# Which expert tiles have their activations worked out ahead: six whole groups, or the first eight tiles and then every third

## The chip, the cores and the metric

The kernel runs on one core of a Trainium2 chip. The metric is the device time of one execution in microseconds (us), lower is better. TensorE (PE) multiplies matrices, VectorE (DVE), ScalarE (ACT) and GpSimd (POOL) work element by element, SyncE (SP) issues most transfers. Each engine takes its own instructions strictly in order and waits on semaphores.

## The reference

Two transformer blocks over 512 tokens of 1024 numbers. The change lies in the expert layer (PEER) of the first block, of which this is the core:

```python
def chunk(xc):                               # 128 tokens at a time
    ...
    idx = jnp.take_along_axis(cidx, fi, axis=-1)     # 8 heads x 16 experts of 16384
    g = jax.nn.softmax(fv, axis=-1)
    u = u_tab[idx]
    a = jax.nn.gelu(jnp.einsum('chkd,cd->chk', u, xc).astype(jnp.float32), approximate=False)
    vv = v_tab[idx]
    return jnp.einsum('chk,chkd->cd', (g * a).astype(vv.dtype), vv)
```

## The kernel before

**Two ways for the experts.** The first 128 tokens are done literally: for each of 128 (head, choice) pairs a row of 1024 numbers per token is gathered from the u table and one from the v table. That makes 256 gathers of 128 rows (512 KB each), issued from POOL (L694) and used on DVE: a u gather by `jk` (L707, a dot product, followed by a short instruction that reads the accumulator), a v gather by `yg` (L709, L711). The other 384 tokens go densely: the 16384 experts are 128 tiles of 128, and for every tile n
- `u_tile(n)` loads 512 KB of the u table, splits it into a high and a low part (`whi` on ACT, L84; `wlo` on DVE, L85), does 24 matmuls (L111) and a Gelu on ACT into a tile `ga` (128 x 384, 192 KB);
- `gated(n)` multiplies `ga` by the gates of its tile on DVE (L755) and splits the product into `wh` (ACT) and `wl` (DVE, L85 too);
- the v part loads 512 KB of the v table, splits it like u, and does 18 matmuls (L782) into six accumulators that stay open over all 128 tiles.

One load and split of 512 KB is called a unit: tile n has a u unit and a v unit. The raw buffers (`wraw`) are a ring of 4 units, `whi` and `wlo` rings of 3.

**Ahead of the loop.** While DVE builds the gate table, PE has room: `ahead(n)` does the u unit of 48 tiles (those of the first six groups of eight). Eight results stay in SBUF (`kept`, tiles 0 to 7), 40 are written to DRAM (`gad`) and read back in the loop by L747, called a reload here. The tiles `ga` are a ring of 8, and a reload into a buffer needs that its last reader is done.

**The loop over n.** Its program order is: v unit of n; u unit or reload of n+2; gates of n+1; v matmuls of n. A scheduler turns that order into a fixed list for each engine at build time, so that instructions of neighbouring tiles interleave. SP's list holds all loads and reloads of the loop: a load that waits for a buffer holds up those behind it. The gates of eight tiles (1536 KB) come by one transfer `gt` from the table `Gd` (L734).

**Pacing the gathers.** After each of the two DVE steps of `gated`, `pace(w, ins)` advances a count by w and lets as many gathers (and, with more than three held, uses) follow `ins` as the count is due:

```python
steps = 8 * VW * GA + 16 * (16 - GA) - 12
...
while done < total * step / steps and gq:
    if len(held) > 3:
        use(ins)
    gather(ins)
    done += 1
```

A tile worked out ahead advances the count by VW = 0.6 in all (two calls of VW/2), any other by 2. `total` is 256.

Of the kernel before, what the change touches and what calls it, by code (L numbers as in the profile page):

```python
# [8 lines left out]
F32 = mybir.dt.float32  # L9
# [11 lines left out]
P = 128  # L21
# [2 lines left out]
KD = D // P  # L24
NTMP = 5
WG = (4, 4, 5)
GAHEAD = 6
KO = (4, 5, 6, 7, 0, 1, 2, 3)
NR = 1
GS = (2, 2, 1, 1)  # L30
# [3 lines left out]
EB, QB, KB, ST = 2, 2, 2, 42  # L34
FA, GA1 = 1.0, 3
SCB = 3
GAB, VW, HB = 8, 0.6, 6
G = 128


# [4 lines left out]
def drain(g):  # L45
    for _ in g:
        pass


class Kern:  # L50
# [383 lines left out]
    def peer(self, h, xg, ss):  # L434

        nc, tc = self.nc, self.tc
        A = self.A
        NB = 3
        ND, T0 = NB * P, P
        TG, NT = 16, NB * P // 16  # L440
        GA = GAHEAD
        st = ExitStack()
        px = st.enter_context(tc.tile_pool(name="px", bufs=1))
        dr = st.enter_context(tc.tile_pool(name="dr", bufs=1, space=DRAM))
        Gd = dr.tile([16, P, NT, 8, TG], F32, name="Gd")
        gad = [dr.tile([P, 8, ND], F32, name=f"gad{n}") for n in range(GA - 1)]
        xtd = px.tile([P, KD, P], F32, name="xtd")
        gid = px.tile([P, P], I32, name="gid")
        gat = px.tile([P, P], F32, name="gat")
# [3 lines left out]
        def ga_tile():  # L453
            return pga.tile([P, ND], F32, name="ga", tag="ga", bufs=GAB)
# [30 lines left out]
        for c in range(2):  # L485
            ps = self.aux().rearrange("p (k d) -> p k d", k=4)
            for k in range(4 * c, 4 * c + 4):
                f = self.t()
# [37 lines left out]
        def route(b):  # L526
# [44 lines left out]
            return terms, g  # L571

        def table(b, terms, g, between):

            rt = rt1
# [42 lines left out]
        def u_tile(n, out):  # L618
            ps = self.mm()[:, :ND]
            self.mm3(ps, self.unit(A["uT"][n], KD), X)  # L620
            nc.scalar.activation(out, ps, AF.Gelu)

        def ahead(n):

            ga, n = ga_tile(), (n + 8) % (GA * 8)
            u_tile(n, ga)
            if n < 8:
                kept.append(ga)
            else:
                nc.sync.dma_start(gad[n // 8 - 1][:, n % 8], ga)  # L630

        kept = []

# [14 lines left out]
        steps, units = 0, 0  # L648
# [3 lines left out]
        def between():  # L652
            nonlocal steps, units
            steps += 1
            if steps in (8, 24):
                routed[steps // 16 + 2] = route(steps // 16 + 2)
            if steps > 32 and steps % 2:
                next(rest, None)
            while units < steps * (GA * 8 - HB) / 48:
                ahead(units)  # L660
                units += 1

        for b in (1, 2, 3):
            table(b, *routed.pop(b), between)
        drain(rest)
        while units < GA * 8:
            ahead(units)
            units += 1
        g_st.close()
# [21 lines left out]
        def gather(after):  # L691
            z, n = gq.pop(0)
            r = pg.tile([P, D], F32, name="gr", tag="gr", bufs=6)
            dep(nc.gpsimd.indirect_dma_start(out=r, out_offset=None, in_=(A["u"], A["v"])[z],  # L694
                                             in_offset=bass.IndirectOffsetOnAxis(ap=gid[:, n:n + 1], axis=0)), after)
            held.append((z, n, r))

        def use(after):
            z, n, r = held.pop(0)
            c = n // 16  # L700
            s16 = slice(16 * c, 16 * c + 16)
            if z == 1 and n % 16 == 0:
                nc.scalar.activation(ag[:, s16], ag[:, s16], AF.Gelu)
                nc.vector.tensor_tensor(ag[:, s16], ag[:, s16], gat[:, s16], op=OP.mult)
            if z == 0:
                jk = pg.tile([P, D], BF, name="jk", tag="jk", bufs=1)
                i = nc.vector.scalar_tensor_tensor(jk, r, 1.0, xf, op0=OP.mult, op1=OP.mult, accum_out=ag[:, n:n + 1])  # L707
            elif n == 0:
                i = nc.vector.tensor_scalar(yg, r, ag[:, n:n + 1], None, op0=OP.mult)  # L709
            else:  # L710
                i = nc.vector.scalar_tensor_tensor(yg, r, ag[:, n:n + 1], yg, op0=OP.mult, op1=OP.add)  # L711
            if after is not None:
                dep(i, after)

        total = len(gq)
        steps = 8 * VW * GA + 16 * (16 - GA) - 12
        done, step = 0, 0.0

        def pace(w, ins):
            nonlocal done, step  # L720
            step += w
# [5 lines that stand above are left out]
# [3 lines left out]
        gts, gas, ws = {}, {}, {}  # L730

        def gates_of(gi):
            gts[gi] = pl.tile([P, NT, 8, TG], F32, name="gt", tag="gt", bufs=2)
            nc.sync.dma_start(gts[gi], Gd[gi])  # L734

        def gelu_u(n):
            gi, i = divmod(n, 8)
            if i == 2 and gi < 15:
                gates_of(gi + 1)
            if n < 8:  # L740
                gas[n] = kept[i]
                return
            ga = gas[n] = ga_tile()
            if gi >= GA:
                u_tile(n, ga)
            else:
                nc.sync.dma_start(ga, gad[gi - 1][:, i])  # L747

        def gated(n):
            gi, i = divmod(n, 8)  # L750
            ga = gas.pop(n)
            wh = pw.tile([P, ND], F32R, name="wh", tag="wh", bufs=3)
            wl = pw.tile([P, ND], F32R, name="wl", tag="wl", bufs=3)
            g3 = ga.rearrange("p (n t) -> p n t", t=TG)
            last = nc.vector.tensor_tensor(g3, g3, gts[gi][:, :, i], op=OP.mult)  # L755
            pace(VW / 2 if gi < GA else 1.0, last)
            last = self.split(ga, wh, wl)
            pace(VW / 2 if gi < GA else 1.0, last)
            ws[n] = wh, wl

        gates_of(0)
        gelu_u(0)
        gelu_u(1)
        gated(0)
        for n in range(P):
            vh, vl = self.unit(A["v"][n * P:n * P + P].rearrange("p (k g) -> p k g", g=G), 8)
            if n + 2 < P:
                gelu_u(n + 2)
            if n + 1 < P:
                gated(n + 1)  # L770
            else:
                assert not gq
                while held:
                    use(None)
                take = self.start2()
            wh, wl = ws.pop(n)
            for f in range(2):
                fs = slice(4 * f, 4 * f + 4)
                for t in range(NB):
                    tk = slice(t * P, t * P + P)  # L780
                    for j, (a, b) in enumerate(((wh, vh), (wh, vl), (wl, vh))):
                        nc.tensor.matmul(acc[f][t], a[:, tk], b[:, fs].rearrange("p k g -> p (k g)"),  # L782
                                         start=n == 0 and j == 0, stop=n == P - 1 and j == 2)
# [917 lines left out]
```

## Time and profile before

| | |
|---|---|
| three timed runs | 2801.33 us median (2794.91 to 2803.78) |
| profiled execution | 2801.58 us, span from first to last instruction 2799.8 us |
| PE busy | 2661.8 us, 95% of the span |
| DVE busy | 1929.1 us, 69% |
| ACT, POOL busy | 1222.7 us, 746.6 us |
| granted TensorE clock, mean | 0.979 of full speed |
| HBM | 158 GB/s over the span |

All times below count from the first instruction of the profiled execution. The expert loop runs from about 770 us to 1679 us. A busy time is that of an engine's instructions; matmuls are pipelined, so the time of a piece of PE work is best read from the start of one piece to the start of the next. "idle before <- X" names what ended an engine's wait.

### The profile page before, as it was taken

The page shows a single profiled execution, that of the slowest core. Times are in us where ns is not written, and L with a number is a line of the kernel's source. Part 1 is how long each engine was busy: PE and PEld are TensorE (multiplying, and loading weights), DVE is VectorE, ACT ScalarE, POOL GpSimd, SP SyncE. Part 2 cuts the span into 40 slices and gives each one's busy share as a digit, 9 for nine tenths or more (in the row PEclk, how much of TensorE's full clock was granted, in tenths as well). Part 3 has the DMA queues.
Part 4 walks back from the last instruction along what each step waited for, and adds up shares of the span by engine and source line. Part 5 has one row for each costly group of instructions (what it writes and reads, how often), then busy time and mean ns, then how long its engine had stood idle before and what let it go on. Part 6 is the DMA issues. An engine that isn't in the chain of part 4 may idle for free.

```text
span 2799.8 us, 38104 instructions
## 1 busy us (share of the span) xinstructions
PE 2661.8 (95%) x13941; PEld 2202.5 (79%) x13941; DVE 1929.1 (69%) x3742; ACT 1222.7 (44%) x2124; POOL 746.6 (27%) x807
## 2 busy tenths in 40 slices
PE   8999999799999999999999998898899989999997
PEld 6777888789987788888888886676667778888886
DVE  4664579997666778887778858877687765545336
ACT  4664354566532333333333336445555545222234
POOL 0100110000022345454545511443544513111002
PEclk9999999899999999999999998999899999999999
DMA  3112322467798878898899952121000013222332
GB/s 122 61 42 76 118 101 84 141 200 241 245 346 288 300 267 324 327 330 314 321 331 332 323 176 91 61 61 46 1 1 1 1 46 107 91 98 91 98 98 76
DMA packets 173356, 446.15 MB, mean 159 GB/s; under 512 B 14192, under 2 KB 76784, under 8 KB 170992
## 3 DMA queue, kind: packets, MB, share of 16 engines
q1 hardware_dynamic: 136304, 309.47, 32.8%
q0 software_dynamic: 36864, 134.23, 13.3%
q8 instruction: 110, 1.80, 0.3%
q14 instruction: 78, 0.64, 0.1%
HBM read 404.33 MB, written 37.22 MB: 158 GB/s over the span
## 4 chain that ended last, share of the span: by engine, by line
PE 69%; DVE 14%; DMA 5%; POOL 4%; issue 4%; ACT 4%; SPq 0%; DVEq 0%; POOLq 0%; ACTq 0%
PE mm L111 46%; PE aux L782 10%; DMA ga<-gad 3%; PE mm L782 2%; DVE wlo L85 2%; PE aux L607 1%; PE mm L1285 1%; PE aux L367 1%; PE aux L325 1%; POOL gl_E L1379 1%; POOL gr L694 1%; PE aux L1212 1%; DVE gl_K L1388 1%; POOL t L915 1%; DMA wraw<-in_v_dram 1%
## 5 line engine op out<-in xcount | busy, mean ns | idle before, releaser
L84 ACT CAST whi<-wraw 128x1024 fp32r<-128x1024 f32 (+2 forms) x439 | 454.1, 1035 | 920.4 <-PE mm L111 764.2
L85 DVE TENSOR_TENSOR wlo<-wraw,whi 128x1024 fp32r<-128x1024 f32 (+2 forms) x439 | 569.1, 1297 | 319.6 <-ACT whi L84 295.9
L111 PE MATMUL mm<-xb,whi 128*128 128x384 f32 (+1 forms) x2656 | 732.8, 356 | 13.9 <-ACT whi L84 13.3
L111 PEld LDWEIGHTS mm<-xb,whi 128*128 128x128 f32 x2656 | 483.6, 190 | 59.2 <-ACT whi L84 28.5
L111 PE MATMUL mm<-xb,wlo 128*128 128x384 f32 (+1 forms) x1328 | 472.8, 356 | 11.7 <-DVE wlo L85 11.7
L694 POOL DMA_INDIRECT gr<-in_u_dram,gid x128 | 192.2, 1501 | 605.3 <-DVE ga L755 495.3
L111 PEld LDWEIGHTS mm<-xb,wlo 128*128 128x128 f32 x1328 | 252.2, 190 | 40.7 <-DVE wlo L85 21.8
L782 PE MATMUL aux<-wlo,wh 128*128 128x512 f32 x640 | 255.4, 399 | 12.3 <-DVE wlo L85 12.2
L694 POOL DMA_INDIRECT gr<-in_v_dram,gid x128 | 194.2, 1517 | 235.3 <-DVE ga L755 106.3
L782 PE MATMUL aux<-whi,wl 128*128 128x512 f32 x640 | 253.4, 396 | 0.0
L782 PE MATMUL aux<-whi,wh 128*128 128x512 f32 x640 | 253.2, 396 | 0.0
L111 PE MATMUL mm<-fx,whi 128*128 128x512 f32 (+1 forms) x736 | 223.2, 386 | 0.0
L111 PE MATMUL mm<-fp,whi 128*128 128x512 f32 (+1 forms) x732 | 200.6, 360 | 1.1 <-ACT fp L84 0.5
L711 DVE SCALAR_TENSOR_TENSOR yg<-gr,ag,yg 128x1024 f32<-128x1024 f32 x127 | 163.1, 1285 | 4.3 <-DMA gr<-in_v_dram,gid 1.8
L707 DVE SCALAR_TENSOR_TENSOR jk<-gr,xtd 128x1024 bf16<-128x1024 f32 x128 | 156.4, 1222 | 9.5 <-DMA gr<-in_u_dram,gid 7.1
L111 PEld LDWEIGHTS mm<-fx,whi 128*128 128x128 f32 x736 | 135.7, 188 | 30.8
L111 PE MATMUL mm<-x,whi 128*128 128x512 f32 x432 | 148.0, 424 | 8.4 <-DVE h L792 7.5
L782 PEld LDWEIGHTS aux<-wlo,wh 128*128 128x128 f32 x640 | 120.5, 188 | 43.1 <-DVE wlo L85 20.0
L111 PEld LDWEIGHTS mm<-fp,whi 128*128 128x128 f32 x732 | 129.6, 189 | 26.3 <-DVE fp L85 1.7
L111 PE MATMUL mm<-fx,wlo 128*128 128x512 f32 (+1 forms) x368 | 141.8, 385 | 0.0
L782 PEld LDWEIGHTS aux<-whi,wl 128*128 128x128 f32 x640 | 120.6, 188 | 24.6
L782 PEld LDWEIGHTS aux<-whi,wh 128*128 128x128 f32 x640 | 120.7, 189 | 24.4
(491 smaller groups left out, 4703.4 us busy)
## 6 DMA issues: line engine op xcount, KB each, us to landing
wraw<-in_uT_dram SPq DMA_DIRECT2D x128, 512.0 KB
wraw<-in_v_dram SPq DMA_DIRECT2D x128, 512.0 KB
wraw<-in_w_in_dram SPq DMA_DIRECT2D x57, 512.0 KB
Gd<-stg SPq DMA_DIRECT2D x24, 1024.0 KB
gt<-Gd SPq DMA_DIRECT2D x16, 1536.0 KB
wraw<-in_ffn_gate_dram SPq DMA_DIRECT2D x22, 512.0 KB
wraw<-in_ffn_up_dram SPq DMA_DIRECT2D x22, 512.0 KB
wraw<-in_ffn_down_dram SPq DMA_DIRECT2D x17, 512.0 KB
```

The costliest lines, as they stand in the source:

```text
L84: self.nc.scalar.copy(hi, src)
L85: return (eng or self.nc.vector).tensor_tensor(lo, src, unr(hi), op=OP.subtract)
L111: self.nc.tensor.matmul(ps, a, b, start=first and n == 1, stop=last and n == 3 * kt)
L325: nc.tensor.matmul(pr[r][:, i, :nk], q[:, hg * 2 + i, b * P:(b + 1) * P], kz[:, r, k0:k0 + nk], start=True, stop=True)
L367: nc.tensor.matmul(po[r * 64:r * 64 + 64], vt[:, k0 // P + kb, r * 64:r * 64 + 64], pT[:, kb], start=kb == 0, stop=kb == nb - 1)
L607: nc.tensor.matmul(ps[:, t], j1[:, z, t4 + t], oi[:, t4 + t], start=z == 0, stop=z == 1)
L694: dep(nc.gpsimd.indirect_dma_start(out=r, out_offset=None, in_=(A["u"], A["v"])[z], in_offset=bass.IndirectOffsetOnAxis(ap=gid[:, n:n + 1] ...
L707: i = nc.vector.scalar_tensor_tensor(jk, r, 1.0, xf, op0=OP.mult, op1=OP.mult, accum_out=ag[:, n:n + 1])
L711: i = nc.vector.scalar_tensor_tensor(yg, r, ag[:, n:n + 1], yg, op0=OP.mult, op1=OP.add)
L782: nc.tensor.matmul(acc[f][t], a[:, tk], b[:, fs].rearrange("p k g -> p (k g)"), start=n == 0 and j == 0, stop=n == P - 1 and j == 2)
L915: nc.gpsimd.tensor_tensor(s, z[:, :T], z[:, 2:], op=OP.add)
L1212: nc.tensor.matmul(ps, BK[:, 0, d], AR[:, :, d], start=True, stop=True)
```

## The change

The same number of u units, 48, is done ahead, but of other tiles: 0 to 7 (kept, as before) and then every third tile of the whole loop, 9, 12, ... 126, 40 in all, each with a DRAM tile of its own. In the loop these 40 are reloaded, the other 80 have their u unit there. A tile done ahead now advances the gathers' count by 1 in place of 0.6 (VW = 0.5, two calls of VW).

```diff
-GAHEAD = 6
-GAB, VW, HB = 8, 0.6, 6
+GAB, VW, HB = 8, 0.5, 6
...
-        gad = [dr.tile([P, 8, ND], F32, name=f"gad{n}") for n in range(GA - 1)]
+        early = [n for n in range(P) if n < 8 or n % 3 == 0]
+        gad = {n: dr.tile([P, ND], F32, name=f"gad{n}") for n in early[8:]}
...
-            ga, n = ga_tile(), (n + 8) % (GA * 8)
+            ga, n = ga_tile(), early[(n + 8) % len(early)]
             u_tile(n, ga)
             if n < 8:
                 kept.append(ga)
             else:
-                nc.sync.dma_start(gad[n // 8 - 1][:, n % 8], ga)
+                nc.sync.dma_start(gad[n], ga)
...
-            while units < steps * (GA * 8 - HB) / 48:
+            while units < steps * (len(early) - HB) / 48:
...
-        steps = 8 * VW * GA + 16 * (16 - GA) - 12
+        steps = 2 * VW * len(early) + 2 * (P - len(early)) - 12
...
             ga = gas[n] = ga_tile()
-            if gi >= GA:
+            if n in gad:
+                nc.sync.dma_start(ga, gad[n])
+            else:
                 u_tile(n, ga)
-            else:
-                nc.sync.dma_start(ga, gad[gi - 1][:, i])
...
-            ga = gas.pop(n)
+            ga, w = gas.pop(n), VW if n in early else 1.0
...
-            pace(VW / 2 if gi < GA else 1.0, last)
+            pace(w, last)
             last = self.split(ga, wh, wl)
-            pace(VW / 2 if gi < GA else 1.0, last)
+            pace(w, last)
```

Every engine has the same instructions before and after, and the same order up to about 775 us and behind the loop; inside the loop they stand in another order. (Line 85 of before is line 84 of the changed kernel, L98 is L97 and L747 is L745.) Two places are shown.

**DVE at the loop's start.** Before: the last u unit done ahead is split between the gate products of tile 3 and of tiles 4 to 6, then the first two v units are split.

```order
L755 TENSOR_TENSOR ga<-ga,gt 128x384
L85 TENSOR_TENSOR wlo<-wraw,whi 128x1024
L755 TENSOR_TENSOR ga<-ga,gt 128x384 x3
L85 TENSOR_TENSOR wlo<-wraw,whi 128x1024 x2
L755 TENSOR_TENSOR ga<-ga,gt 128x384
```

Changed:

```order
L755 TENSOR_TENSOR ga<-ga,gt 128x384
L84 TENSOR_TENSOR wlo<-wraw,whi 128x1024
L707 SCALAR_TENSOR_TENSOR jk,ag<-gr,xtd 128x1024
L755 TENSOR_TENSOR ga<-ga,gt 128x384 x3
L84 TENSOR_TENSOR wlo<-wraw,whi 128x1024 x2
L755 TENSOR_TENSOR ga<-ga,gt 128x384
```

The use of the first gather has moved ahead of the first split of a v unit.

**SP and DVE around the reload of tile 24.** On SP before, `ga_8303`, `ga_8338` and `ga_8369` are the tiles 22, 23 and 24, the `wraw` the v units of 18, 19 and 20:

```order
L747 DMA ga_8303<-gad1_2849 128x384
L98 DMA wraw_8227<-in_v_dram 128x1024
L747 DMA ga_8338<-gad1_2849 128x384
L98 DMA wraw_8262<-in_v_dram 128x1024
L747 DMA ga_8369<-gad2_2850 128x384
L734 DMA gt_8439<-Gd_2847 128x3072
L98 DMA wraw_8297<-in_v_dram 128x1024
```

On DVE before, `wl_8129` is the split of the product of tile 16, which gives back the buffer that tile 24 is reloaded into; `ga_8369` is the gate product of tile 24, and `wlo_8194` the split of the v unit of 17:

```order
L85 TENSOR_TENSOR wl_8129<-ga_8095,wh_8128 128x384
L755 TENSOR_TENSOR ga_8338<-ga_8338,gt_7883 128x384
L85 TENSOR_TENSOR wlo_8157<-wraw_8155,whi_8156 128x1024
L755 TENSOR_TENSOR ga_8369<-ga_8369,gt_8161 128x384
L85 TENSOR_TENSOR wl_8166<-ga_8126,wh_8165 128x384
L85 TENSOR_TENSOR wlo_8194<-wraw_8192,whi_8193 128x1024
```

On SP changed, `ga_8827` is tile 24; the rows ahead of it are the v units of 23 and 22, u of 25, v of 24 and u of 26:

```order
L97 DMA wraw_8860<-in_v_dram 128x1024
L97 DMA wraw_8821<-in_v_dram 128x1024
L97 DMA wraw_8868<-in_uT_dram 128x1024
L97 DMA wraw_8930<-in_v_dram 128x1024
L97 DMA wraw_8940<-in_uT_dram 128x1024
L745 DMA ga_8827<-gad24_2853 128x384
L97 DMA wraw_9002<-in_v_dram 128x1024
```

On DVE changed, `wlo_8757` is the split of the u unit of 23, which frees the raw buffer that the u load of 26 ahead of the reload waits for; `wlo_8932` is the split of the v unit of 24:

```order
L84 TENSOR_TENSOR wlo_8757<-wraw_8755,whi_8756 128x1024
L707 SCALAR_TENSOR_TENSOR jk_8799,ag_7636<-gr_8661,xtd_2888 128x1024
L84 TENSOR_TENSOR wlo_8870<-wraw_8868,whi_8869 128x1024
L755 TENSOR_TENSOR ga_8753<-ga_8753,gt_7973 128x384
L707 SCALAR_TENSOR_TENSOR jk_8832,ag_7636<-gr_8727,xtd_2888 128x1024
L84 TENSOR_TENSOR wl_8830<-ga_8753,wh_8829 128x384
L84 TENSOR_TENSOR wlo_8862<-wraw_8860,whi_8861 128x1024
L707 SCALAR_TENSOR_TENSOR jk_8838,ag_7636<-gr_8791,xtd_2888 128x1024
L755 TENSOR_TENSOR ga_8827<-ga_8827,gt_8468 128x384
L84 TENSOR_TENSOR wlo_8932<-wraw_8930,whi_8931 128x1024
```

Before, the reload of tile 24 is released by `wl` of tile 16; two DVE instructions stand between that and the product of tile 24, and the split of v 17 stands behind it. Changed, it is released by the split of u 23; seven DVE instructions stand between, and the split of v 24 right behind the product.

## Rows read from the trace of the kernel before

**Rows 1.** Windows: busy us (instructions) per engine, clock, DMA share, GB/s.

```profile
780.90:992.90 212.00, 199.67 (x832) 155.54 (x831) 142.80 (x195) 68.45 (x94) 58.43 (x38) 0.99 0.83 305
992.90:1679.00 686.10, 683.93 (x3398) 603.70 (x3398) 531.48 (x652) 241.40 (x333) 322.37 (x214) 1.00 0.85 306
```

**Rows 2.** Chain that ended last, pieces in order: start us, us, what.

```profile
980.26 3.50 PE aux L782 x15
983.76 0.70 PE mm L782 x3
...
992.88 4.17 PE mm L111 x24
```

**Rows 3.** Waits, 780.9 to 992.9: us in total, times, longest us.

```profile
DVE ga L755 <- DMA ga<-gad: 52.9, 22, 5.1
PEld aux L782 <- DVE wlo L85: 20.0, 18, 3.1
```

**Rows 4.** Waits of SP's own queue, 780.9 to 992.9.

```profile
SPq L747 <- DVE wl L85: 59.0, 23, 6.4
```

**Rows 5.** Timeline of SP's queue, 838 to 866: start us, us.

```profile
848.12 0.32 SPq L747 DMA_DIRECT2D ga<-gad  x1
```

**Rows 6.** Timeline of DVE, 846 to 866.

```profile
847.53 0.56 DVE L85 TENSOR_TENSOR wl<-ga,wh 128x384 fp32r<-128x384 f32 x1
848.08 0.56 DVE L755 TENSOR_TENSOR ga<-ga,gt 128x384 f32<-128x384 f32 x1
848.55 1.22 DVE L85 TENSOR_TENSOR wlo<-wraw,whi 128x1024 fp32r<-128x1024 f32 x1
854.89 0.56 DVE L755 TENSOR_TENSOR ga<-ga,gt 128x384 f32<-128x384 f32 x1 [5.12 <-DMA ga<-gad]
```

**Rows 7.** Timeline of PE, 853 to 862.

```profile
857.11 0.49 PE L782 MATMUL aux<-wlo,wh 128*128 128x512 f32 x1 [1.93 <-DVE wlo L85]
```

**Rows 8.** Waits, 992.9 to 1679.

```profile
ACT whi L84 <- PE mm L111: 343.9, 77, 10.2
```

**Rows 9.** Groups by line, 1000 to 1640: xcount | busy us, mean ns | idle before.

```profile
L85 DVE TENSOR_TENSOR wlo<-wraw,whi 128x1024 fp32r<-128x1024 f32 x151 | 184.5, 1222 | 114.3 <-ACT whi L84 108.8 <-PE mm L782 5.4
...
L711 DVE SCALAR_TENSOR_TENSOR yg<-gr,ag,yg 128x1024 f32<-128x1024 f32 x112 | 143.8, 1284 | 4.1 <-DMA gr<-in_v_dram,gid 1.8
L707 DVE SCALAR_TENSOR_TENSOR jk<-gr,xtd 128x1024 bf16<-128x1024 f32 x106 | 129.5, 1222 | 7.0 <-DMA gr<-in_u_dram,gid 5.0
...
L707 DVE DVE_READ_ACCUMULATOR jk<-gr,xtd 128x1 f32 x106 | 8.7, 82 | 0.0
```

**Rows 10.** Windows around 888, as rows 1, and PE's timeline at 1276.

```profile
888.00:891.00 3.00, 3.00 (x9) 2.32 (x8) 2.16 (x3) 0.00 (x0) 0.00 (x0) 0.50 0.66 200
...
1276.24 0.44 PE L111 MATMUL mm<-xb,wlo 128*128 128x384 f32 x1 [2.17 <-DVE wlo L85]
```

**Rows 11.** Chain that ended last: two of its 15 reloads.

```profile
822.79 7.16 DMA ga<-gad
...
865.30 2.32 DMA ga<-gad
```

**Rows 12.** Gathers' queue, 776.2 to 779.6: packets, MB, share; a window as rows 1.

```profile
q0 software_dynamic: 144, 0.52, 51.9%
...
810.00:820.00 10.00, 9.99 (x44) 7.73 (x43) 8.20 (x14) 3.50 (x6) 0.00 (x0) 1.00 1.04 409
```

**Rows 13.** Timelines at the loop's start: POOL, then DVE, then PE.

```profile
774.00 1.51 POOL L694 DMA_INDIRECT gr<-in_u_dram,gid  x1 [373.81 <-DVE ga L755]
...
775.80 1.22 DVE L85 TENSOR_TENSOR wlo<-wraw,whi 128x1024 fp32r<-128x1024 f32 x1
776.93 1.49 DVE L755 TENSOR_TENSOR ga<-ga,gt 128x384 f32<-128x384 f32 x3
779.83 1.23 DVE L85 TENSOR_TENSOR wlo<-wraw,whi 128x1024 fp32r<-128x1024 f32 x1 [1.41 <-ACT whi L84]
...
781.30 0.39 PE L782 MATMUL aux<-wlo,wh 128*128 128x512 f32 x1
```

More of the change, by code (lines that the diff above doesn't have):

```diff
@@ L440, in peer @@
         TG, NT = 16, NB * P // 16
-        GA = GAHEAD
         st = ExitStack()
@@ L665, in peer @@
         drain(rest)
-        while units < GA * 8:
+        while units < len(early):
             ahead(units)
```

## The prediction

> **What bounds the kernel now.** I read the windows of the expert loop first, as the diff touches nothing else, and split them where PE starts its first u unit inside the loop, at 992.9 us. Ahead of that only v units run (u was done ahead), behind it u and v alternate. The reader should see two regimes [rows 1]: in the second stretch PE is busy 683.9 of 686.1 us, in the first 199.7 of 212.0, while DVE is busier in the second (77%) than in the first (67%). So PE bounds the second stretch, and something that is not throughput holds up the first.
>
> The chain of waits gives the size of a unit for PE: a v unit takes 3.50 + 0.70 = 4.20 us where nothing stalls, a u unit 4.17 us [rows 2]. The first stretch holds the v units of tiles 0 to 45: 46 x 4.20 = 193.2 us of 212.0, so **18.8 us** are lost. The second holds 82 v and 80 u units: 344.4 + 333.6 = 678.0 of 686.1, 8.1 us lost.
>
> The waits tell what loses them. In the first stretch DVE waited 52.9 us in 22 places for the reload of `ga`, up to 5.1 us each, and PE's weight loads waited 20.0 us for `wlo`, DVE's half of a split [rows 3]. SP in turn waited 59.0 us for `wl`, until it could issue reloads [rows 4]. That is a ring: a reload needs the buffer that `wl` of the tile eight before gives back, and DVE has its product almost at once. Tile 24 shows one turn: `wl` of tile 16 ends at 848.1 [rows 6], SP issues the reload at 848.12 [rows 5], DVE has two more instructions (0.56 and 1.22 us) and then waits 5.12 us [rows 6]; the split of v 17, which stands behind, reaches PE at 857.11 after 1.93 us of idle [rows 7]. The product is of tile 24 and needed only seven v units later; it costs time because DVE takes instructions in order. In the second stretch the wait points the other way: ACT's casts wait 343.9 us for PE to free `whi` [rows 8].
>
> **What the change does, part by part.**
>
> *Units.* 48 u units ahead, 80 in the loop, 40 writes and 40 reloads: all as before. Ahead of the loop every engine's order is the same, so that stretch costs nothing new. PE's work in the loop stays 128 x 4.20 + 80 x 4.17 = 871.2 us; before, the loop took 212.0 + 686.1 = 898.1, so 26.9 us is all that can be had.
>
> *DVE's load.* A use costs on average (1.22 + 0.08 + 1.28) / 2 = 1.29 us, a split of a unit 1.22 [rows 9], a product or `wl` 0.56 [rows 6]. Before, the gathers' count ends at 8 x 0.6 x 6 + 16 x 10 - 12 = 176.8, so a tile with u in the loop takes 2 x 256 / 176.8 = 2.90 gathers and DVE needs 2 x 1.22 + 2 x 0.56 + 2.90 x 1.29 = 7.3 of PE's 8.37 us, 87%. This ran without idle on PE. Changed, the count ends at 2 x 0.5 x 48 + 2 x 80 - 12 = 196: 1.31 gathers for a tile done ahead, 2.61 for another. The repeating piece is one tile of the first kind and two of the other: 5 splits, 6 small steps, 6.53 uses, 6.1 + 3.4 + 8.4 = 17.9 us on DVE against 3 x 4.20 + 2 x 4.17 = 20.9 on PE, 85%. In bytes it is 5 x 512 + 4 x 192 + 6.53 x 512 = 6671 KB, 319 per us; the second stretch before needs (2 x 512 + 192 + 2.90 x 512) / 8.37 = 323. So the whole loop becomes a little lighter than a stretch in which PE was never the one to wait for long.
>
> *Reloads.* One in three tiles, the ring of eight no longer turns on them. In the new order SP's reload stands behind unit loads, and its product on DVE stands four to eight instructions after the split that frees those loads. Counted for all 40 with the durations above, these are 3.5 to 7.6 us of DVE work (tile 24: three uses, two splits, two small steps, 3.9 + 2.4 + 1.1 = 7.4). A reload took 2.32 to 7.16 us [rows 11]. The rest of a wait falls into DVE's spare 3.0 us per three tiles. The trace shows no reload in the mixed stream, so I bound it: below, no stall at all; above, each reload keeps what it costs PE now, 18.8 / 40 = 0.47 us. I take the lower end, since the row it is nearest to is the second stretch's: PE busy 99.7%. The 8.1 us lost there I carry over by length, 8.1 x 871.2 / 678.0 = 10.4 us.
>
> By the Trainium skill, "DMA: Bandwidth & Descriptors", section "Anatomy of one DMA — SWDGE (gpsimd) path", a transfer takes about 2.0 us and its bytes at 436 GB/s, which makes an estimated 2.45 us for a reload of 196,608 bytes; then no reload of the changed kernel could be late, and the upper bound would fall away. The rows differ, up to 7.16 us, and I go by them.
>
> *Loop start.* The higher count puts the first use ahead of the first split of a v unit. The first gather is issued at 774.00 [rows 13]; its 144 packets, 0.52 MB, pass between 776.2 and 779.6 [rows 12]. DVE is done with the last u split at 775.80 + 1.22 = 777.0 [rows 13], and would now wait to 779.6, do the use (1.30, to 780.9), three products (1.49, to 782.4) and only then the split of v 0 (1.22, to 783.6). Now that split runs at 779.83, to 781.06, and PE's second v matmul, which needs it, at 781.30 [rows 13]. So PE stalls 783.7 - 781.3 = **2.4 us** here. The nearest stalls of that size: 2.17 us at 1276 [rows 10], behind which matmuls ran slow, and a longer one ahead of 888, where the clock was granted at 0.50 (1.2 instead of 2.4 GHz) for 3 us [rows 10]. Such a dip costs 1.7 us (3.4 us at half speed, taking its edges in); the 1.93 us at 857 [rows 7] had none. I take half, 0.8, and keep 0 and 1.7.
>
> The start also moves more bytes. Up to the tenth v unit the count now asks for 9 x 1.31 + 2.61 = 14.4 gathers where it was 10 x 0.87 = 8.7, and two u units come in (8 and 10), against eight reloads of 0.2 MB that fall away: 5.7 x 0.52 + 2 x 0.52 - 1.6 = 2.4 MB. The queues have moved 409 GB/s in a stretch of 10 us [rows 12], so this is 6 us at most, if PE had to wait for all of it, and nothing if the ring of four units covers it. I take nothing: in the first stretch now PE's waits are for splits that DVE was late with, in a load as heavy as this.
>
> **Sum.** Against the profiled execution, 2801.6 us (the median of the three runs is 2801.3, so no correction): 2801.6 - 898.1 + 871.2 + 10.4 + 2.4 + 0.8 = **2788.3 us**, 0.5% less.
>
> **The rivals.**
>
> *Reloads stay late (no change).* For it: SP's reload now stands behind the u load of two tiles further on and is wanted by the very next v unit, where the old product had seven tiles to spare; 40 reloads remain. Kept in full, the time is 2801.6 + 2.4 + 0.8 = 2804.8; with half kept about 2795. Against it: the cover of 3.5 to 7.6 us where it was 1.8 for tile 24.
>
> *DVE becomes the bound (slower).* One mechanism: the in-order wait for reloads grows past the spare time. The piece of three tiles costs DVE 17.9 us and the wait; it passes PE's 20.9 at a wait of 3.0 per reload, and the kernel gets slower than before at about 3.6, where 40 x 0.6 us eat the 26.9 - 2.4 that could be had. With 4.0 it is 40 x (21.9 - 20.9) = 40 us: 2801.6 - 26.9 + 2.4 + 40 = 2817. The first stretch had 52.9 / 40 = 1.3 us per reload with less cover.
>
> *Nothing new is lost.* PE is held nowhere but at the start: 2801.6 - 26.9 + 2.4 = 2777.
>
> **How the numbers follow.** Chances: the forecast (2781 to 2795) 0.60, late reloads with a time within 2795 to 2807 0.24, slower by DVE 0.07, nothing lost (2777 to 2781) 0.09. 0.3%, or 8.4 us, is about what a measurement tells from no change here (the three runs spread over 8.9 us): faster means below 2792.9. Of the forecast's 0.60 some 0.02 lies above that; faster 0.67, same 0.25, slower 0.08 (the DVE case and a little of the late reloads). The range 2778 to 2803 leaves out the slower case, the top of the late reloads and the very bottom, under 0.2 together.
>
> **What would show it.** From 781 to the loop's end the time falls from 898 to about 885; PE has no long row of waits for `wlo` up to 992.9, and in every window of the loop runs u and v units in the ratio 2 to 3. DVE's wait for `ga<-gad` falls well below 52.9 us, SP's wait of L745 for `wl` to nearly nothing. At 777 DVE waits about 2.6 us for the first gather, and PE 2.4 us for the split of v 0. Wrong it would be if PE's waits for `wlo` came back once in three tiles, or if ACT's casts waited for `wraw` loads instead of PE in the first 50 us.

## The result, and the profile after

| | before | after |
|---|---|---|
| median | 2801.14 us (2794.91 to 2803.78) | 2823.64 us (2816.95 to 2827.85) |
| profiled execution | 2801.58 us, span 2799.8 | 2816.95 us, span 2815.2 |
| loop, first to last v matmul | 897.8 us | 916.8 us |
| the rest of the span | 1902.0 us | 1898.4 us |

The change made the kernel slower: 1.0087 times the time before, 95% interval 1.0067 to 1.0106, where I had forecast 0.995. The loop alone took 19.0 us more; I had expected 13.3 less of it.

Windows of the changed kernel, for the whole loop and for its two parts (us, busy us and instructions of PE, PEld, DVE, ACT and POOL, clock, DMA share, GB/s), against [rows 1]:

```profile
780.40:1697.20 916.80, 887.00 (x4225) 769.92 (x4225) 672.26 (x848) 314.12 (x427) 387.55 (x252) 0.99 0.83 299
780.40:1000.00 219.60, 213.05 (x1009) 184.04 (x1009) 163.41 (x207) 75.49 (x102) 94.94 (x63) 0.99 0.86 313
1000.00:1697.20 697.20, 673.95 (x3218) 585.88 (x3217) 508.86 (x642) 238.63 (x325) 292.61 (x190) 0.99 0.82 295
```

The first stretch is no longer the bad one: PE is idle for 3% of it, where it was 6%. But the idleness now runs through the whole loop, 29.8 us of 916.8, and 23 us of it lie behind 1000 us, where PE had waited some 2 us in all. DVE is no busier than before (672 us, and 674 in [rows 1] together).

The waits of the changed kernel, 780 to 1700 us (us in total, times, longest), against [rows 3, 8]:

```profile
ACT whi L83 <- PE mm L110: 260.0, 65, 8.9
...
ACT whi L83 <- DMA wraw<-in_v_dram: 61.3, 14, 6.9
...
DVE ga L755 <- DMA ga<-gad: 24.6, 10, 3.6
PEld mm L110 <- ACT whi L83: 24.4, 26, 4.7
PEld mm L110 <- DVE wlo L84: 19.1, 19, 2.4
PE mm L110 <- ACT whi L83: 16.5, 11, 4.3
...
PE mm L110 <- DVE wlo L84: 11.2, 12, 1.9
```

The old wait has halved: DVE waited 52.9 us for reloads, now 24.6. A new one stands first among the transfers: ACT's casts wait 61.3 us for raw weights of v units (5.9 us before), and PE waits 16.5 + 11.2 = 27.7 us at u units (`mm L110`), for both halves of their split; before, it had one such wait in the loop, the 2.17 us at 1276 [rows 10].

One such place, read engine by engine. Timelines of the changed kernel around the v unit of 34 and the u unit of 35; first SP and DVE, then ACT, then PE (L782 are v matmuls, L110 u matmuls):

```profile
995.90 0.33 SPq L97 DMA_DIRECT2D wraw<-in_v_dram  x1
...
992.94 1.28 DVE L711 SCALAR_TENSOR_TENSOR yg<-gr,ag,yg 128x1024 f32<-128x1024 f32 x1
994.15 0.55 DVE L84 TENSOR_TENSOR wl<-ga,wh 128x384 fp32r<-128x384 f32 x1
994.62 1.22 DVE L84 TENSOR_TENSOR wlo<-wraw,whi 128x1024 fp32r<-128x1024 f32 x1
...
1003.33 1.05 ACT L83 CAST whi<-wraw 128x1024 fp32r<-128x1024 f32 x1 [5.24 <-DMA wraw<-in_v_dram]
1004.29 0.48 ACT L621 ACTIVATE ga<-mm 128x384 f32<-128x384 f32 x1
1006.14 0.51 ACT L83 CAST wh<-ga 128x384 fp32r<-128x384 f32 x1 [1.37 <-DVE ga L755]
1006.56 1.04 ACT L83 CAST whi<-wraw 128x1024 fp32r<-128x1024 f32 x1
...
1005.46 0.40 PE L782 MATMUL aux<-whi,wl 128*128 128x512 f32 x1
1007.65 0.61 PE L110 MATMUL mm<-xb,whi 128*128 128x384 f32 x2 [1.79 <-ACT whi L83]
...
1010.35 0.45 PE L110 MATMUL mm<-xb,wlo 128*128 128x384 f32 x1 [0.70 <-DVE wlo L84]
```

The split of v 32 (DVE at 994.62) ends at 995.84 and frees one of four raw buffers. At 995.90 SP issues the load of v 34 into it. The cast of v 34 is the next in ACT's list, and ACT takes its instructions in order: it stands idle 5.24 us until that load is there, at 1003.3. (Some 2 us of this it would have waited anyhow, until PE ends u 34 at 1000.3 and with it frees a `whi` buffer.) SP had issued another v load 3.4 us earlier, at 992.47, that of v 35, which ACT casts only behind u 35. Then follow the cast of v 34, a Gelu, the cast of a gate product, and only then, at 1006.56, the cast of u 35, whose own load had landed at 986.8. PE has two u matmuls of tile 35 in the middle of v 33 and waits 1.79 us for the cast and 0.70 for the rest of the split. Matching PE's gaps with ACT's rows ahead of them, 25.6 of 31.7 us of gaps at u units (start to start, less the usual step) have the cast of a late v load just ahead of the u cast in ACT's list.

In some of these places the v load is late because a reload was late first. One of them, DVE's rows and then ACT's:

```profile
908.20 0.56 DVE L755 TENSOR_TENSOR ga<-ga,gt 128x384 f32<-128x384 f32 x1 [3.57 <-DMA ga<-gad]
...
909.82 1.22 DVE L84 TENSOR_TENSOR wlo<-wraw,whi 128x1024 fp32r<-128x1024 f32 x1
...
904.51 1.05 ACT L83 CAST whi<-wraw 128x1024 fp32r<-128x1024 f32 x1 [1.06 <-PE mm L782]
...
915.06 1.05 ACT L83 CAST whi<-wraw 128x1024 fp32r<-128x1024 f32 x1 [4.80 <-DMA wraw<-in_v_dram]
```

The cast at 904.51 is done at 905.56, but the other half of its split stands behind a gate product that waits 3.57 us for its reload, and begins at 909.82. The v load that gets the freed buffer is issued at 911.07; ACT waits 4.80 us for it, and PE then 0.93 + 0.87 us at a u unit. Followed back like this, 5 of the 11 places where PE waits at a u unit behind a late v load begin with a late reload; PE waits 10.6 us in these and 11.9 us in the other six.

The loop's start went as worked out from [rows 13]. DVE, then PE, then two windows, of the changed kernel:

```profile
778.95 1.23 DVE L707 SCALAR_TENSOR_TENSOR jk<-gr,xtd 128x1024 bf16<-128x1024 f32 x1 [3.03 <-DMA gr<-in_u_dram,gid]
...
781.50 1.22 DVE L84 TENSOR_TENSOR wlo<-wraw,whi 128x1024 fp32r<-128x1024 f32 x1
...
780.40 0.40 PE L782 MATMUL aux<-whi,wh 128*128 128x512 f32 x1
782.78 0.50 PE L782 MATMUL aux<-wlo,wh 128*128 128x512 f32 x1 [1.98 <-DVE wlo L84]
...
784.00:787.50 3.50, 3.50 (x10) 2.70 (x10) 2.12 (x3) 1.04 (x1) 0.00 (x0) 0.53 1.03 418
...
1579.50:1586.30 6.80, 5.33 (x13) 4.13 (x14) 5.21 (x7) 1.41 (x3) 2.62 (x2) 0.50 0.53 163
```

DVE waits 3.03 us for the first gather, PE starts its second v matmul 2.38 us after its first, and the half clock (1.2 GHz) follows at 784. The last window is one of two more such dips, behind the longest of the new waits.

### The profile page after: what moved, and what is told of

The parts are those of the page before. It is cut to its first block, busy times and chain, and to the rows that moved or that the text cites. A ratio compares the mean times of both kernels' runs of the same rounds, so it can differ in the third digit from the quotient of the medians.

```text
span 2815.2 us, 38087 instructions
## 1 busy us (share of the span) xinstructions
PE 2662.0 (95%) x13941; PEld 2209.4 (78%) x13941; DVE 1924.1 (68%) x3742; ACT 1227.5 (44%) x2124; POOL 755.5 (27%) x807
## 5 line engine op out<-in xcount | busy, mean ns | idle before, releaser
L110 PE MATMUL mm<-xb,whi 128*128 128x384 f32 (+1 forms) x2656 | 733.6, 357 | 29.8 <-ACT whi L83 28.7
L110 PEld LDWEIGHTS mm<-xb,whi 128*128 128x128 f32 x2656 | 487.1, 190 | 72.5 <-ACT whi L83 38.4
L110 PE MATMUL mm<-xb,wlo 128*128 128x384 f32 (+1 forms) x1328 | 472.8, 356 | 21.5 <-DVE wlo L84 21.5
L694 POOL DMA_INDIRECT gr<-in_u_dram,gid x128 | 198.0, 1547 | 605.7 <-DVE ga L755 531.4
L110 PEld LDWEIGHTS mm<-xb,wlo 128*128 128x128 f32 x1328 | 252.1, 190 | 46.0 <-DVE wlo L84 31.0
L782 PE MATMUL aux<-wlo,wh 128*128 128x512 f32 x640 | 255.2, 399 | 2.0 <-DVE wlo L84 2.0
L782 PE MATMUL aux<-whi,wl 128*128 128x512 f32 x640 | 254.1, 397 | 0.0
L782 PE MATMUL aux<-whi,wh 128*128 128x512 f32 x640 | 254.0, 397 | 0.0
L110 PE MATMUL mm<-fx,whi 128*128 128x512 f32 (+1 forms) x736 | 223.1, 386 | 0.0
L110 PE MATMUL mm<-fp,whi 128*128 128x512 f32 (+1 forms) x732 | 200.6, 361 | 1.0 <-ACT fp L83 0.5
L110 PEld LDWEIGHTS mm<-fx,whi 128*128 128x128 f32 x736 | 135.7, 188 | 30.7
L110 PE MATMUL mm<-x,whi 128*128 128x512 f32 x432 | 144.2, 414 | 9.0 <-DVE h L792 7.5
L110 PEld LDWEIGHTS mm<-fp,whi 128*128 128x128 f32 x732 | 129.6, 189 | 26.2 <-DVE fp L84 1.6
L782 PEld LDWEIGHTS aux<-whi,wl 128*128 128x128 f32 x640 | 121.1, 189 | 27.7
L782 PEld LDWEIGHTS aux<-wlo,wh 128*128 128x128 f32 x640 | 121.0, 189 | 27.1 <-DVE wlo L84 2.4
L110 PE MATMUL mm<-fx,wlo 128*128 128x512 f32 (+1 forms) x368 | 141.8, 385 | 0.0
L782 PEld LDWEIGHTS aux<-whi,wh 128*128 128x128 f32 x640 | 121.2, 189 | 25.2
```

The costliest lines, as they stand in the source:

```text
L110: self.nc.tensor.matmul(ps, a, b, start=first and n == 1, stop=last and n == 3 * kt)
```

## The experiments

Theory 1: a v load is issued too late, because its raw buffer is freed too late, and the next u unit's cast stands behind it. Rivals: the reloads and gathers slow or delay the transfers (theory 2); the split buffers are what is scarce (theory 3); the new weights did it, not the choice of tiles (theory 4). Ratios are to the kernel before, timed beside each.

**e1_raw5: five raw buffers.**

```diff
-        raw, hi, lo = buf("wraw", F32, 2, 2), buf("whi", F32R, 2, 1), buf("wlo", F32R, 2, 1)
+        raw, hi, lo = buf("wraw", F32, 2, 3), buf("whi", F32R, 2, 1), buf("wlo", F32R, 2, 1)
```

> The changed kernel with five raw weight buffers in place of four (the second pool's share goes from 2 to 3), nothing else. Theory 1 (late v load): after the change the loads of neighbouring v and u units stand swapped in SP's list, a v load is issued only when the split two units earlier has freed its raw buffer, it lands after ACT should have cast it, and the cast of the next u unit, whose own load landed about 20 us earlier, stands behind it in ACT's list. One more raw buffer lets the load be issued about a unit (some 7 us) earlier, about the time it takes to land; the stalls of this kind sum to 25.6 us in the trace of the changed kernel, so the time should fall by 18 to 26 us, to about 2791 to 2799 (ratio to the kernel before 0.997 to 0.999), and ACT's wait for raw v data, 61.3 us in the loop, should fall under 20. Theory 2 (the reloads and the gathers now share the transfers and slow them): a transfer is as slow as before, the time stays above 2810. Theory 3 (the scarce resource is the split buffers, not the raw ones): no change, 2817 or more.

2786.77 us, ratio 0.9946 [0.9933, 0.9959]. 37 us off the changed kernel's time, more than expected, with every reload and every gather still there. Its loop as a window, and its waits:

```profile
780.30:1665.80 885.50, 877.37 (x4226) 766.24 (x4225) 672.06 (x850) 315.69 (x427) 390.17 (x252) 1.00 0.86 310
...
PEld mm L110 <- DVE wlo L84: 9.1, 14, 1.6
PEld mm L110 <- ACT whi L83: 7.2, 27, 1.4
ACT whi L83 <- DMA wraw<-in_v_dram: 7.1, 3, 4.9
```

The wait for raw v data went from 61.3 to 7.1 us, PE's idle time from 29.8 to 8.1. DVE still waits 26.5 us for reloads here, about as long as after the change. The loop of 885.5 us is the one that the prediction had worked out for the change (871.2 + 10.4 + 2.4 + 0.8 = 884.8). At the same place ACT casts v 34 with no wait for its load, and u 35 follows in time:

```profile
995.06 1.05 ACT L83 CAST whi<-wraw 128x1024 fp32r<-128x1024 f32 x1 [2.08 <-PE mm L110]
...
1000.63 0.52 PE L110 MATMUL mm<-xb,whi 128*128 128x384 f32 x2
```

**e2_hi4: four split buffers, four raw ones.**

```diff
-        raw, hi, lo = buf("wraw", F32, 2, 2), buf("whi", F32R, 2, 1), buf("wlo", F32R, 2, 1)
+        raw, hi, lo = buf("wraw", F32, 2, 2), buf("whi", F32R, 2, 2), buf("wlo", F32R, 2, 2)
```

> The changed kernel with four buffers for each split weight half (whi, wlo) in place of three, raw buffers as they are. Theory 1 (late v load): the split of a unit may run one unit ahead, so its raw buffer is freed earlier and the next load is issued earlier; TensorE has a whole unit of work in hand when a cast is late, in place of the 1.40 us seen at u35. Time down by 15 to 27 us, to 2790 to 2802. Theory 3 (split buffers are what is scarce): the same fall here, but none with a fifth raw buffer. Theory 2 (slower transfers): what is late stays late on average, at most 10 us gained, above 2807.

2783.78 us, ratio 0.9935 [0.9922, 0.9948]. This works as well; theory 3, by which a raw buffer would have been useless, falls with e1. ACT still waits 15.4 us for raw v data here, and DVE even 50.1 us for reloads, twice as long as after the change, yet PE's waits at u units are 7.7 us where they were 27.7. Either buffer gives the loads more lead, the time from the instruction that frees a buffer to the one that needs its next load.

**e3_noreload: no reloads.**

```diff
-            if n in gad:
-                nc.sync.dma_start(ga, gad[n])
-            else:
+            if n not in gad:
                 u_tile(n, ga)
...
-            last = nc.vector.tensor_tensor(g3, g3, gts[gi][:, :, i], op=OP.mult)
+            g1 = gts[gi][:, :, i]
+            last = nc.vector.tensor_tensor(g3, g1 if n in gad else g3, g1, op=OP.mult)
```

> The changed kernel without its 40 reloads of early results: for those tiles the gate product multiplies the gates by themselves, so that it waits for no transfer (the output is therefore another). Theory 2 (reloads slow or delay what TensorE needs, in the queue or in the transfers): 20 to 32 us faster than the changed kernel, 2785 to 2797. Theory 1 (late v load behind the raw buffers): at most the 24.6 us of VectorE's waits for reloads go, none of which was TensorE's to wait for; the stalls at u units inside v units remain, 2808 to 2820.

2789.51 us, ratio 0.9952 [0.9939, 0.9965]. As theory 2 had it, and a miss of theory 1 by some 19 us. The waits do not fit either theory:

```profile
ACT whi L83 <- DMA wraw<-in_v_dram: 50.5, 13, 5.4
PEld mm L110 <- ACT whi L83: 7.0, 21, 1.2
PEld mm L110 <- DVE wlo L84: 3.7, 11, 0.4
```

The v loads are late nearly as often and as long as after the change (50.5 us), yet PE waits only 1.6 us at u units. So a late v load alone is not enough. Taking the reloads out does three things: their bytes are gone, no gate product waits for one, and the scheduler writes other lists. e9 and e13 put the bytes back alone.

**e4_vw03: the old weight, 0.3 a step.**

```diff
-GAB, VW, HB = 8, 0.5, 6
+GAB, VW, HB = 8, 0.3, 6
```

> The changed kernel with the early tiles' weight in the interleaving as it was (0.3 a step in place of 0.5); the choice of tiles stays every third. Theory 1: the stall at the loop's start (2.4 us of waiting and about 1.7 us of half clock) goes, since the first gather use stands behind the first v splits again; the swapped pairs of loads come from the mixture of u units among v units, so most of the 25.6 us stay: 2805 to 2815. Theory 4 (the new weights alone put the u units where they stall): most of the 31.7 us of loop stalls go, 2785 to 2795.

2821.14 us, ratio 1.0060 [1.0043, 1.0077]. PE's wait at the loop's start went (0.8 us are left) and ACT's wait for raw v data stayed, 67.3 us. PE's waits at u units are 27.4 us, as after the change. The weight did not make the stalls; theory 4 falls for the mixed loop. DVE's waits for reloads are shorter here, 16.6 us, and stand at the head of only 3 of 12 such places: the stalls do not need a late reload. The time missed theory 1's range by 6 us.

**e5_poolreload: the reloads on GpSimd's queue.**

```diff
-                nc.sync.dma_start(ga, gad[n])
+                nc.gpsimd.dma_start(ga, gad[n])
```

> The changed kernel with its 40 reloads issued from GpSimd's queue in place of SyncE's; the lists of TensorE, ScalarE and VectorE are the same row for row, SP's is the old one without the reloads, and the same bytes move. Without the reloads at all (e3) the time fell to 2789.5, but there the three engines' lists had moved as well. Theory 1 (a v load is issued only when the split that frees its raw buffer has run): the reload's place in SP's list is no part of it, time 2810 to 2824, ACT's waits for raw v data about 61 us as before. Theory 2 (a reload ahead of the v load in SP's queue shares its time of transfer and makes it late): time 2788 to 2800, ACT's waits for raw v data under 40. Against both: a reload issued behind GpSimd's gathers comes late itself, VectorE then waits for reloads over 40 us and the time is above 2825.

2826.90 us, ratio 1.0091 [1.0073, 1.0108], the changed kernel's ratio again (3 us above theory 1's range, in that of the third expectation, whose sign, over 40 us of waits for reloads, did not show). The lists of PE, ACT and DVE are the changed kernel's row for row, which makes the two easy to compare. Its waits:

```profile
ACT whi L83 <- DMA wraw<-in_v_dram: 58.0, 14, 7.1
DVE ga L755 <- DMA ga<-gad: 32.9, 10, 5.0
PEld mm L110 <- ACT whi L83: 28.5, 26, 4.0
```

The reload's place in SP's queue does not matter, and the reloads themselves came late by little more than before (32.9 us, not over 40).

**e6_first48: the old choice of tiles, all else changed.**

```diff
-        early = [n for n in range(P) if n < 8 or n % 3 == 0]
+        early = [n for n in range(P) if n < 48]
```

> The changed kernel with the tiles worked ahead chosen as before the change (the first 48); the reload by tile, the separate buffers and the weight of 0.5 a step stay as changed. Theory 1 (the mixture of the two sorts of tile makes the stalls): stretches are pure again, the stalls at u units inside v units go, the waits for reloads come back: 2795 to 2808. Theory 4 (the weights and the machinery): 2812 to 2825.

2813.60 us, ratio 1.0051 [1.0035, 1.0067]: theory 1's range is missed, theory 4's holds. In the pure first stretch the weight does matter, or else that each reload now has a DRAM tile of its own; no run tells these two apart. Its waits, 779 to 1000 us:

```profile
DVE ga L755 <- DMA ga<-gad: 57.2, 23, 6.5
PEld aux L782 <- DVE wlo L84: 33.8, 14, 6.0
```

PE's waits behind the old kind of late reload grew from 20.0 us [rows 3] to 33.8, with the clock's mean at 0.95 in the first 212 us of the loop, where it was 0.99 [rows 1]. More gathers in that stretch stand in DVE's list between the reloads.

**e7_raw5_hi4: both buffers.**

```diff
-        raw, hi, lo = buf("wraw", F32, 2, 2), buf("whi", F32R, 2, 1), buf("wlo", F32R, 2, 1)
+        raw, hi, lo = buf("wraw", F32, 2, 3), buf("whi", F32R, 2, 2), buf("wlo", F32R, 2, 2)
```

> The changed kernel with five raw and four split buffers. Theory 1: both remove the same wait (each alone took 30 to 33 us off the loop, 916.8 to 885.5 and 888.0), so together they give at most a few us more than one: 2776 to 2787. If they were cures of two separate waits: under 2770.

2785.76 us, ratio 0.9944 [0.9929, 0.9959]: no more than one of them alone. They cure the same wait.

**e8_before_raw5: the edit of e1 in the kernel before.**

> The kernel before the change with five raw buffers, as a control. Theory 1: the late v load was made by the change, so a fifth buffer gives the kernel before little: its first stretch waits for reloads as before (20.0 us of TensorE's weight loads behind VectorE), its second loses 8.1 us in all: 2793 to 2803, and the changed kernel with the same buffer (2786.8) is the faster of the two by 6 to 16 us, which is the size forecast for the change. If a raw buffer is worth about 30 us to either kernel: 2770 to 2780, and the change is a loss with it too.

2794.25 us, ratio 0.9974 [0.9962, 0.9986], 6 us and not 37. `PEld aux L782 <- DVE wlo` is 20.0 us in 18 places there too, as in [rows 3]. The need for the fifth buffer came with the change.

**e9_sparereload and e13_spaced_spare: e3 with the bytes put back.** In both, each of the 40 reloads goes into a tile that nobody reads; in e13 it also waits (`dep`) for the last split of the gated tile two before.

```diff
+            if n in gad:
+                dep(nc.sync.dma_start(pl.tile([P, ND], F32, name="dg", tag="dg", bufs=2), gad[n]), lasts[-1])
```

> The kernel of e3 (no product waits for a reload; for those tiles the gates are multiplied by themselves, so the output is another), but with the 40 reloads issued at their old places into a spare tile that nobody reads. The lists of TensorE and VectorE are those of e3, the bytes moved are those of the changed kernel. If e3's gain of 34 us came from the lists (without the reload the scheduler sets the split that frees a raw buffer ahead of the gather's sum in VectorE's list): 2786 to 2796. If it came from 7.9 MB less to move: 2810 or more.

e9: 2807.06 us, ratio 1.0022 [1.0011, 1.0034], between the two. It doesn't tell what it was meant to. The spare reloads' rows in SP's queue, SP's wait at them (798 to 872 us), one v load, and ACT's cast of it:

```profile
L745 SPq DMA_DIRECT2D dg<-gad x34: 319/320/956, 798.9 to 871.1; - x34
...
SPq L745 <- DMA dg<-gad: 49.7, 25, 6.3
...
855.23 0.56 SPq L97 DMA_DIRECT2D wraw<-in_v_dram  x1
...
862.56 1.04 ACT L83 CAST whi<-wraw 128x1024 fp32r<-128x1024 f32 x1 [9.69 <-DMA wraw<-in_v_dram]
```

All 40 were issued by 871 us, six of them ahead of 770. The spare tile has two buffers, so each waits until the spare reload two before it has landed: that held SP 49.7 us in 25 places, and the loads behind with it; one v load came so late that ACT waited 9.69 us, and PE about as long.

> As e9 (e3's products without a reload, so another output, and the 40 reloads into a spare tile), but each spare reload waits for the gate product and split two tiles earlier, so that they are spread over the loop, one in each third tile, where e9 had them all crowded into the first tiles. The lists of TensorE, ScalarE and VectorE are those of e3. If e3's gain came from these lists: 2786 to 2797, TensorE's waits at u units under 15 us. If it came from the bytes that no longer move: 2808 to 2824, TensorE's waits at u units over 30 us. Between the two, both have a part.

e13: 2791.58 us, ratio 0.9971 [0.9962, 0.9980], with the reloads spread over the loop. Their rows, and its waits:

```profile
L746 SPq DMA_DIRECT2D dg<-gad x40: 326/327/337, 804.1 to 1639.8; - x40
...
ACT whi L83 <- DMA wraw<-in_v_dram: 67.4, 18, 5.2
PEld mm L110 <- ACT whi L83: 8.7, 21, 1.3
PEld mm L110 <- DVE wlo L84: 3.8, 12, 0.5
```

The bytes are back and the time is that of e3 within 0.2%. So it was not the traffic, and theory 2 falls. What e3 and e13 share against the changed kernel is the lists of PE, ACT and DVE, and that no product waits for a reload. How the lists differ is seen on DVE at the split of v 32, in e3, against the changed kernel's rows above:

```profile
990.51 1.22 DVE L84 TENSOR_TENSOR wlo<-wraw,whi 128x1024 fp32r<-128x1024 f32 x1
991.64 1.28 DVE L711 SCALAR_TENSOR_TENSOR yg<-gr,ag,yg 128x1024 f32<-128x1024 f32 x1
992.84 0.55 DVE L84 TENSOR_TENSOR wl<-ga,wh 128x384 fp32r<-128x384 f32 x1
```

Here the split stands ahead of the gather's sum and `wl`; after the change it stands behind them. From the end of this split to PE's first matmul of v 33, 10.0 us pass in e3 (991.73 to 1001.74), and 8.4 us in the changed kernel (995.84 to 1004.29): the load of v 34 is late by less, as PE counts it, and the next u cast is almost in time. Pairing casts and splits in their order, 790 to 1640 us, DVE's half begins on average 0.37 us after the cast ends in e3, 0.38 in e13 and 0.93 in the changed kernel. There, the ten that stand behind a product waiting for its reload begin 3.3 us after it, the other 183 0.80 us: the order of the list and the late reloads both hold the splits back.

**e10_raw5_vw03, e11_raw5_first48, e12_raw6: what is left with five raw buffers.** e10 and e11 are e1 with the edits of e4 and e6; e12 has six raw buffers (`buf("wraw", F32, 2, 4)`).

> The changed kernel with five raw buffers and the early tiles' weight back at 0.3 a step. With the raw buffers out of the way the wait at the loop's start is the largest that is left (2.6 us in e1, 0.8 in e4): if the two are apart, 2 to 4 us less than e1, 2782 to 2785. If the weight matters in the mixed loop as it does in pure stretches (e6 lost 12 us on it), 2770 to 2778.

2779.77 us, ratio 0.9920 [0.9904, 0.9937], the lowest ratio of all: 0.8% faster than the kernel before, 1.7% (0.9920 / 1.0087) than the changed one. The gain over e1 was expected at 2 to 4 us and came out at 7, but the two intervals overlap, and the profiled loops differ by 2.3 us (883.2 and 885.5), which is what the start is worth:

```profile
782.20:1665.40 883.20, 876.68 (x4225) 763.87 (x4224) 672.15 (x846) 315.31 (x427) 381.45 (x252) 1.00 0.87 311
```

> The first 48 tiles worked ahead as in e6, weight 0.5 a step, with five raw buffers. In e6 TensorE waits in the first stretch, 33.8 us of weight loads behind splits, where VectorE waits for reloads and has the gathers of a weight of 0.5 to add up. If that is VectorE's in-order list and not the raw ring: 2806 to 2815, 20 us and more above e1 with the same weight and buffers, which is what the mixture itself then gives. If the raw ring is behind it there too: 2785 to 2795.

2811.57 us, ratio 1.0036 [1.0024, 1.0048]: a raw buffer does little for the pure stretch (e6 was 1.0051), where the reloads are what is late (`DVE ga <- DMA` 53.6 us).

> The changed kernel with six raw buffers. Theory 1: five were enough to issue each v load before its cast is due (ACT's waits for raw v data fell from 61.3 to 7.1 us), a sixth has some 7 us of such waits and 10 us of TensorE's left to take: 2780 to 2788. If lateness of loads still sets the time with five: under 2778.

2790.40 us, ratio 0.9961 [0.9948, 0.9975]: no gain over five, 2 us above theory 1's range; ACT's wait for raw v data is 6.9 us, as in e1.

Together, as ratios (the first 48 tiles at 0.3 with four buffers are the kernel before itself, whose reloads are cut by group but move the same bytes):

| tiles ahead, weight a step | four raw buffers | five |
|---|---|---|
| first 48, 0.3 | 1 | 0.9974 |
| first 48, 0.5 | 1.0051 | 1.0036 |
| 8 and every third, 0.3 | 1.0060 | 0.9920 |
| 8 and every third, 0.5 | 1.0087 | 0.9946 |

The sign of the change hangs on one buffer. With five raw buffers the choice of tiles at 0.3 gives 0.9920 / 0.9974 = 0.9946, about 15 us; the change as it was made gives 0.9946 / 0.9974 = 0.9972, 8 us. With four, the choice of tiles at 0.3 costs 0.6%, and the change as it was made 0.9%.

## Why the prediction was wrong

**The first stretch: right.** PE's waits for `wlo` at v units went (20.0 us, then 2.4, all at the start), DVE's for reloads fell from 52.9 to 24.6 us, and SP's queue has no wait at its reload line left (59.0 us in [rows 4]).

**The start: right.** 2.4 us of PE's time forecast; the second v matmul comes 2.38 us after the first, 2.15 more than the usual step. The dip of the clock, taken at half its price, came in full: 1.7 us in place of 0.8.

**DVE's load: right.** 85% of PE's time was worked out for the repeating piece; windows of 100 us in e1 show 73 to 81%, a little less. DVE's throughput is not the bound, and that rival did not occur.

**The reloads: right in size, wrong in where they cost.** DVE's waits for them fell as forecast, and PE has no wait at a v unit left but the one at the start. But "the rest of a wait falls into DVE's spare 3.0 us per three tiles" counted DVE's time and not what stands behind the product in its list: a split that frees a raw buffer. That is the way the five places above take to PE.

```profile
wraw<-in_v_dram SPq DMA_DIRECT2D x116, 512.0 KB, 5.8
...
ga<-gad SPq DMA_DIRECT2D x38, 192.0 KB, 7.2
```

These are the changed kernel's loads and reloads from 790 to 1640 us, with the median from issue to landing. By the Trainium skill, "DMA: Bandwidth & Descriptors", "Anatomy of one DMA — SWDGE (gpsimd) path", a reload was estimated at 2.45 us. That section is on transfers issued from GpSimd, and SP issues the reloads; in e5, where GpSimd issues them, the median is 7.2 us too, so going by the rows was right.

**The step that failed: "The 8.1 us lost there I carry over by length, 8.1 x 871.2 / 678.0 = 10.4 us".** It takes the second stretch's rate of loss as a property of mixed u and v work. By the waits, what lay behind that rate was the lead of its loads in its lists: in that stretch `ACT whi <- DMA wraw<-in_v_dram` is a small matter (5.9 us in 4 places for the whole loop before), though a u cast there has no more slack: counted through the order with the rows' durations, PE has 1.3 to 1.6 us of other work ahead of its use, and 1.4 us at u 35 after the change. In the new mixture of two v units and a u unit, then a v and a u, loads are issued in another order, a v load comes after the next tile's u load, and a ring of four gives it no lead. In place of 10.4 us stood 916.8 - 871.2 - 2.4 - 1.7 = 41.5; 27.7 of them are PE's waits at u units, and some 4 the two later stretches at half clock. The same thought stands in the sentence on the start, "nothing if the ring of four units covers it. I take nothing": the ring was named, and its lead was not measured. Bytes per us (319 against 323) and DVE's share were the wrong things to compare, since both are averages and the loss is one of lead. With a fifth buffer the forecast's sum holds: a loop of 884.8 us forecast, 885.5 measured, and 2786.8 us in all against 2788.3. That the total agrees so well is in part luck: e1's loop has no stretch at half clock (0.8 in the sum), loses 11.7 us beside the start where 10.4 stood, and the rest of its profiled span is 6 us shorter than before.

**What would have shown it.** The prediction's last sentence named the sign, ACT's casts waiting for `wraw` loads, but looked for it in the first 50 us only, and it gave the case no price among the rivals. The order after the change was at hand: in it the v loads of 23 and 22 stand swapped, with u 25 behind. Following one raw buffer through it would have given the lead: between the split of v 32, which frees it, and the cast of v 34, which needs the next load, only two casts (1.06 and 0.52 us) stand in ACT's list, and in the changed kernel's trace loads around there took 4.3 to 8.4 us.

**Open.** How much of e3's gain belongs to the order of its lists, and how much to the waits for reloads that are gone, was not told apart; no run keeps the changed kernel's lists with reloads that come in time. The span outside the loop varies by some 13 us from one profiled execution to another (1895.6 us in e1, 1903.6 in e10, 1908.9 in e5) with no cause found; the ratios include it.

## What to carry to other kernels

A stretch that runs without waits gives a rate only for its own order of work. Before such a rate is carried to a new order, follow one buffer of each ring through the new lists, from the instruction that frees it to the one that needs the next load, and compare that time with the longest loads in the trace, not with the mean rate. Where a change of order comes out slower with the same work, try one more buffer in the ring that the loads wait for before undoing the order: here that turned 0.9% lost into 0.5% won (0.3% against the kernel before with the same buffer).

## What the runs showed of the hardware

In the changed kernel the granted clock fell to half for 3.4 us behind a PE gap of 2.38 us (start to start, at 780.4), for 3.4 us behind one of 3.25 us (at 1265.4), and for 6.8 us behind one of 4.67 us (at 1576.3), and not behind one of 2.33 us at 1468.3. The length of the gap alone does not settle it: at the loop's start, a gap of 2.84 us in e2 was followed by a clock of 0.51 from 785.2 to 788.6, and one of 2.81 us in e1 was not. So a gap of PE near that size costs its own length, and in some cases 1.7 us more.

In the changed kernel's loop (309 GB/s from 790 to 1640 us) the small transfer was not the quicker one: a reload of 192 KB took 7.2 us from issue to landing, a load of 512 KB 5.8 us (v) or 6.2 us (u), in the median.
